# A DeltaNet scan that takes the state's part from the values before the inverse is applied, in three steps between thirds of projections

## The chip, the cores and the metric

The kernel runs on one core of one Trainium2 chip. The metric is device time in microseconds (us), from the start of the program to its end on that core. Each kernel is run several times; the median counts, and one further execution is profiled.

## The reference, cut to what matters

The reference is one layer of a decoder on 1,024 tokens of width 1,024: a gated DeltaNet with 8 heads of width 128, a sparse attention, two gates and a feed-forward part. The change touches the DeltaNet. Each head works through its sequence in chunks and hands a 128 x 128 state from chunk to chunk:

```python
kb = k * beta[..., None]
vb = v * beta[..., None]
a = jnp.where(strict, jnp.einsum('nbhid,nbhjd->nbhij', kb, k) * decay, 0.0)
t_mat = a + jnp.eye(C, dtype=f32)
u = lax.linalg.triangular_solve(t_mat, vb, left_side=True, lower=True)
w = lax.linalg.triangular_solve(t_mat, kb * jnp.exp(gc)[..., None], left_side=True, lower=True)
...
def step(state, inp):
    qd, ke, u_c, w_c, qk_c, gl = inp
    v_new = u_c - jnp.einsum('bhcd,bhde->bhce', w_c, state)
    o = jnp.einsum('bhcd,bhde->bhce', qd, state) + jnp.einsum('bhij,bhje->bhie', qk_c, v_new)
    state = state * gl[..., None, None] + jnp.einsum('bhcd,bhce->bhde', ke, v_new)
    return state, o
```

Both `u` and `w` are the inverse of `t_mat` times something. So `v_new` is also the inverse times (`vb` minus the decayed keys, scaled by beta, times the state).

## The kernel before, in words

The kernel uses chunks of 128 tokens, so a head has 8 chunks, in two halves of four. TensorE multiplies in two kinds. The projections split each float32 operand into a rounded part and a rest (`hh`, `hl` of the input, `wh`, `wl` of the weights) and add three products for each of 8 slices of the contraction; a half of one projection is 24 such products of 128 x 512 into one PSUM tile `g`. The DeltaNet's own products are 128 x 128 in plain float32; the trace has two records for each of them.

All work up to the sparse attention is entered in a list `due` by `at(step, rank, function)`, sorted by step and rank, and recorded in that order; a scheduler then settles the order on each engine. One step holds one half of a projection. `head(h, s0)` enters one head: four projections (k, q, v and the gate z) in steps `s0` to `s0 + 8`, the preparation of keys, decays and the triangular inverse beside them, the inverse's last parts up to `s0 + 15`, then `u_w` at `s0 + 15.5`, the 8 calls of `chunk` half a step apart from `s0 + 16`, and the output's norm and turn (`out_norm`, `out_turn`). The next head begins at `s0 + 14`, after six steps of other projections (`fill_nb`, four steps with 256-wide products, and one `fill_rows`, two steps). So the chunks of a head stand among the next head's projections and its key preparation. The last head's chunks stand among the remaining `fill_rows`. At step `END` the pools of this stage are closed and those of the sparse attention are opened (`tail_c`, `sparse_setup`); its items begin around `FULL`.

In `u_w`, `zs` (the inverse, transposed) is multiplied with `vb` to `u` and with `kbe` to the first half of `wq`; the second half of `wq` is the query times the decays, which GpSimd computes in `k_q`. In `chunk`, TensorE multiplies `wq` with the state `St` (two products), DVE (VectorE) forms `vn` as `u` minus the first, TensorE multiplies `ke` with `vn`, DVE updates the state, and TensorE adds `qk` times `vn` to the second product. TensorE runs its instructions in their order, so a product behind `ke` waits when `vn` is late. DVE does too. The norm of the keys (`k_natural`) goes from DVE to GpSimd for a power (`rsqrt`, line 239) and back to DVE for `nat`, and DVE's later rows stand behind `nat`.

Of the kernel before, what the change touches and what calls it, by code (L numbers as in the profile page):

```python
# [19 lines left out]
S = 1024  # L20
# [123 lines left out]
def body(ctx: ExitStack, tc: tile.TileContext, A, out):  # L144
# [246 lines left out]
    eg = PL.cq.tile([128, 8, NT], F32, name="eg")  # L391
# [3 lines left out]
    beg = PL.cq.tile([128, 8, NT], F32, name="beg")  # L395

    def gating():
# [44 lines left out]
        act(eg, gc, AF.Exp)  # L442
        V.tensor_tensor(beg, beta, eg, OP.mult)
# [187 lines left out]
    def head(h, s0):  # L631
# [11 lines left out]
        def conv(s, half):  # L643

            c0 = 20 + (s * 8 + h) * 4
            ps = H.pop("g")
            proj(ps, H["w", s], half, (4, 8))
# [30 lines left out]
        def k_turn(half):  # L678
# [6 lines left out]
            kb = t4("kbe", 2)  # L685
            rows_by(kb, kn, beg[:, h, sl])
            H["kbe", half] = kb
# [5 lines left out]
            H["qk", half] = dt = t4("qk", 3)  # L693
# [59 lines left out]
        def k_q(half):  # L753
            ac = H.pop(("ac", 0, half))
            dt = H["qk", half]
            V.tensor_tensor(dt, dt, four(H["kT", half], ac), OP.mult)
            w = pd.tile([128, 4, 2, 128], F32, name="wq", bufs=2)
            GP.tensor_tensor(w[:, :, 1], ac, H["gcB"].rearrange("p (t c) -> p t c", c=128)[:, S4[half]],
                             OP.mult)
            H["wq", half] = w  # L760

        def v_natural(half):
            ps = flip(H.pop(("ac", 2, half)))
            v_ = t4("vb", 2)
# [3 lines left out]
        def first(s, half):  # L768
            H["g"] = gtile()
            proj(H["g"], H["w", s], half, (0, 4))  # L770

        def gate(half):
            ps = H.pop("g")
            proj(ps, H["w", 3], half, (4, 8))
# [56 lines left out]
        def u_w(half):  # L831
            u = t2("u", 2)
            act(u, four(zs[half], H["vb", half]))
            H["u", half] = u
            act(H["wq", half][:, :, 0], four(H["kbe", half], zs[half]))

        def chunk(c):
# [40 lines left out]
        for i, s in enumerate((1, 0, 2, 3)):  # L878
            at(s0 + 2 * i - 2, 2, prep, s)
            for half in range(2):  # L880
                at(s0 + 2 * i + half, 1, first, s, half)
                if s < 3:
                    at(s0 + 2 * i + half + 0.5, 1, conv, s, half)
                else:
                    at(s0 + 2 * i + half + 0.5, 1, gate, half)
        for half in range(2):
# [12 lines left out]
            at(s0 + 15.5, 0, u_w, half)  # L899
        at(s0 + 5, -1, row_decay)  # L900
        at(s0 + 6.5, 0, blocks)
        for c in range(8):
            at(s0 + 16 + c / 2, -2, chunk, c)
        at(s0 + 19, -1, out_norm, 0)
        at(s0 + 20, -1, out_turn, 0)
        at(s0 + 21.2, -1, out_norm, 1)
        at(s0 + 22.2, -1, out_turn, 1)

    def fill_rows(src, dst):
# [6 lines left out]
        def begin(half):  # L916
            w[1] = gtile()
            proj(w[1], w[0], half, (0, 4))

        def go(half):  # L920
            ps = w[1]
            proj(ps, w[0], half, (4, 8))
# [5 lines left out]
        def plan(s, half):  # L928
            at(s, 1, begin, half)
            at(s + 0.5, 1, go, half)  # L930
# [3 lines left out]
    def fill_nb(u):  # L934
# [11 lines left out]

        def go(t):
            tk = slice(t * 128, (t + 1) * 128)
            ps = gtile(256)
            gemm(ps, [(hh[:, k, tk], hl[:, k, tk], w[k // 2][0][:, k % 2], w[k // 2][1][:, k % 2])  # L950
                      for k in range(8)])
# [28 lines left out]
        def plan(s, j):  # L980
            for t in (2 * j, 2 * j + 1):
                at(s + t % 2 / 2, 1, go, t)
# [8 lines left out]
    for h in range(NDN):  # L991
# [3 lines left out]
        fills = gts if h == 7 else nbs[6:] if h == 6 else [nbs[h], gts.pop(0)]  # L995
# [5 lines left out]
    END, FULL = last + 24, last + 28  # L1001
# [769 lines left out]
```

## Time and profile before

| | |
|---|---|
| Median of 3 runs | 2360.92 us (2360.64 to 2361.92) |
| The profiled execution's own time | 2355.1 us |
| Its span in the trace | 2353.3 us |
| TensorE (PE) busy | 2306.0 us, 98% |
| DVE busy | 1567.3 us, 67% |
| ScalarE (ACT) busy | 1155.6 us, 49% |
| GpSimd (POOL) busy | 184.2 us, 8% |
| Mean granted clock | 0.997 of full speed |

The span covers the recorded instructions; the profiled execution lasted 1.8 us longer, and the median of the timed runs is 5.8 us above that execution. The DeltaNet's heads take the trace from about 60 to 1035 us. The page counts a product as busy until its modelled end, which overlaps the next product's start. What one product costs in a row of products is therefore the distance between starts, not the duration shown.

### The profile page before, as it was taken

The page shows a single profiled execution, that of the slowest core. Times are in us where ns is not written, and L with a number is a line of the kernel's source. Part 1 is how long each engine was busy: PE and PEld are TensorE (multiplying, and loading weights), DVE is VectorE, ACT ScalarE, POOL GpSimd, SP SyncE. Part 2 cuts the span into 40 slices and gives each one's busy share as a digit, 9 for nine tenths or more (in the row PEclk, how much of TensorE's full clock was granted, in tenths as well). Part 3 has the DMA queues.
Part 4 walks back from the last instruction along what each step waited for, and adds up shares of the span by engine and source line. Part 5 has one row for each costly group of instructions (what it writes and reads, how often), then busy time and mean ns, then how long its engine had stood idle before and what let it go on. Part 6 is the DMA issues. An engine that isn't in the chain of part 4 may idle for free.

```text
span 2353.3 us, 43197 instructions
## 1 busy us (share of the span) xinstructions
PE 2306.0 (98%) x16257; PEld 1917.6 (81%) x16257; DVE 1567.3 (67%) x3742; ACT 1155.6 (49%) x2482; POOL 184.2 (8%) x198
## 2 busy tenths in 40 slices
PE   8999999999999999999999999999999999999999
PEld 5888988888988898886777777778878888888887
DVE  7676654747574748247777777645498777787775
ACT  4335353535444454337666666532465555544443
POOL 1021210101111121000010111100000000000000
PEclk9999999999999999999999999999999999999999
DMA  6421313131213221247342422065525443595333
GB/s 196 122 62 59 81 52 96 47 89 47 84 47 84 59 74 55 82 143 184 109 128 63 122 87 66 19 220 166 174 90 179 148 148 131 189 327 185 115 114 103
DMA packets 237378, 267.28 MB, mean 114 GB/s; under 512 B 76848, under 2 KB 128496, under 8 KB 237040
## 3 DMA queue, kind: packets, MB, share of 16 engines
q1 hardware_dynamic: 237168, 264.51, 36.1%
q8 instruction: 128, 2.10, 0.4%
q14 instruction: 82, 0.67, 0.1%
HBM read 190.02 MB, written 72.38 MB: 112 GB/s over the span
## 4 chain that ended last, share of the span: by engine, by line
PE 86%; DVE 6%; DMA 2%; issue 2%; ACT 1%; POOL 1%; SPq 0%; ACTq 0%; POOLq 0%; DVEq 0%
PE g L174 31%; PE V L174 20%; PE Q L174 12%; PE T L174 5%; PE s L174 5%; PE o L174 5%; PE S L174 2%; PE c L174 2%; PE m L174 1%; POOL ss L239 1%; PE tp L606 1%; DVE wl L274 1%; PE tp L174 1%; DVE junk L1238 0%; DVE acc L659 0%
## 5 line engine op out<-in xcount | busy, mean ns | idle before, releaser
L174 PE MATMUL g<-hh,wh 128*128 128x512 f32 (+1 forms) x816 | 335.9, 412 | 6.6 <-ACT hh L171 6.5
L174 PE MATMUL g<-hl,wh 128*128 128x512 f32 (+1 forms) x816 | 322.8, 396 | 0.1
L174 PE MATMUL g<-hh,wl 128*128 128x512 f32 (+1 forms) x816 | 322.4, 395 | 0.0
L171 ACT ACTIVATE wh<-a 128x512 fp32r<-128x512 f32 x234 | 146.5, 629 | 252.9 <-PE V L174 154.4
L174 PE MATMUL V<-big,wh 128*128 128x512 f32 x768 | 236.7, 390 | 0.8 <-DVE c L1613 0.8
L1238 DVE CUSTOM_DVE_ANT_0 junk<-S,cst 128x384 f32<-128x384 f32 (+3 forms) x320 | 168.5, 533 | 57.9 <-PE S L174 53.7
L171 ACT ACTIVATE P<-T 128x512 f32<-128x512 f32 x228 | 133.8, 597 | 102.1 <-PE T L174 89.3
L174 PEld LDWEIGHTS g<-hh,wh 128*128 128x128 f32 (+1 forms) x816 | 154.1, 189 | 36.4 <-ACT hh L171 7.1
L171 ACT ACTIVATE wh<-wr 128x512 fp32r<-128x512 f32 x168 | 105.7, 629 | 158.6 <-PE g L174 126.9
L183 DVE TENSOR_TENSOR wl<-a,wh 128x512 fp32r<-128x512 f32 x192 | 132.0, 690 | 75.2 <-ACT wh L171 74.9
L174 PEld LDWEIGHTS g<-hh,wl 128*128 128x128 f32 (+1 forms) x816 | 153.8, 188 | 33.7 <-issue 0.6
L174 PEld LDWEIGHTS g<-hl,wh 128*128 128x128 f32 (+1 forms) x816 | 154.3, 189 | 28.7 <-DVE hl L327 1.5
L174 PEld LDWEIGHTS V<-big,wh 128*128 128x128 f32 x768 | 144.1, 188 | 31.4 <-DVE c L1613 1.2
L174 PE MATMUL V<-big,wl 128*128 128x512 f32 x384 | 149.5, 389 | 0.9 <-DVE wl L274 0.9
L174 PE MATMUL g<-wh,hh 128*128 128x256 f32 x512 | 148.8, 291 | 0.3 <-DVE acc L777 0.3
L174 PE MATMUL g<-wl,hh 128*128 128x256 f32 x512 | 145.4, 284 | 0.0
L174 PE MATMUL g<-wh,hl 128*128 128x256 f32 x512 | 144.7, 283 | 0.0
L174 PEld LDWEIGHTS o<-vv,P 128*64 128x64 f32 x3648 | 115.9, 138 | 27.0 <-issue 19.4
L174 PE MATMUL o<-vv,P 128*64 128x65 f32 x3648 | 129.9, 225 | 0.6 <-DVE bs L1285 0.6
L274 DVE TENSOR_TENSOR wl<-wr,wh 128x512 fp32r<-128x512 f32 x136 | 94.1, 695 | 52.5 <-ACT wh L171 46.8
L174 PE MATMUL S<-ks,qc 96*128 96x384 f32 (+3 forms) x320 | 126.4, 407 | 1.0 <-DVE mx L1238 0.4
L174 PE MATMUL Q<-big,wh 128*128 128x512 f32 x384 | 118.4, 390 | 0.7 <-ACT wh L171 0.5
(383 smaller groups left out, 5348.9 us busy)
## 6 DMA issues: line engine op xcount, KB each, us to landing
bb<-acd SPq DMA_DIRECT2D x112, 256.0 KB, 2.7
wr<-in_w_dn_dram SPq DMA_DIRECT2D x64, 256.0 KB, 3.0
a<-in_w_u_dram SPq DMA_DIRECT2D x64, 256.0 KB, 2.7
acd<-c SPq DMA_DIRECT2D x64, 256.0 KB, 2.1
a<-in_w_d_dram SPq DMA_DIRECT2D x64, 256.0 KB, 3.7
wr<-in_w_nb_dram SPq DMA_DIRECT2D x32, 256.0 KB, 2.6
wr<-in_w_gt_dram SPq DMA_DIRECT2D x32, 256.0 KB, 2.8
gtd<-fx SPq DMA_DIRECT2D x32, 256.0 KB, 2.4
```

Of the source, the lines that this page charges most:

```text
L171: return SC.activation(o, i, fn, **kw)
L174: return PE.matmul(o, l, r, start=start, stop=stop, skip_group_check=True)
L183: V.tensor_tensor(lo, src, f(hi), OP.subtract)
L239: GP.tensor_tensor(o, o, mhalf[:ss.shape[0], :n], OP.pow)
L274: V.tensor_tensor(wl, wr, f(wh), OP.subtract)
L606: PE.transpose(pt[:, i, :], src[:, i, :], ident)
L1238: V.tensor_tensor_reduce(junk[:, :w], ps[:, :w], mask[:, a:b], 1.0, 3e38, OP.add, OP.min, o)
```

## The change

`u_w` goes, and with it `u`, `kbe` and the query half of `wq` on GpSimd. Two tiles come instead, both made on DVE in `k_q`: `kg`, the transposed keys times the decays, and `qg`, the queries times the decays. A chunk is now three functions. `chunk_keys` multiplies `kg` with the state, and DVE forms `t` as that times beta minus `vb`. `chunk_values` multiplies the inverse `zs` with `t`, and ACT copies the negated result to `vn`. `chunk_out` does the products with `ke`, `qg` and `qk` and updates the state. Each half projection is cut into 9, 9 and 6 products where it was 12 and 12, and the three functions stand between these parts. A chunk takes one step, not half a step. The output's norm and turn, `END` and `FULL` come later by one to three steps within the head, head 0 loses its `fill_rows` and the last head has one more.

```diff
-            kb = t4("kbe", 2)
-            rows_by(kb, kn, beg[:, h, sl])
-            H["kbe", half] = kb
...
-            w = pd.tile([128, 4, 2, 128], F32, name="wq", bufs=2)
-            GP.tensor_tensor(w[:, :, 1], ac, H["gcB"].rearrange("p (t c) -> p t c", c=128)[:, S4[half]],
-                             OP.mult)
-            H["wq", half] = w
+            for n, x in (("kg", H["kT", half]), ("qg", ac)):
+                H[n, half] = w = t4(n, 2 if n == "kg" else 3)
+                V.tensor_tensor(w, x, H["gcB"].rearrange("p (t c) -> p t c", c=128)[:, S4[half]], OP.mult)
...
-        def first(s, half):
-            H["g"] = gtile()
-            proj(H["g"], H["w", s], half, (0, 4))
+        def first(s, half, k):
+            if k == 0:
+                H["g"] = gtile()
+            proj(H["g"], H["w", s], half, (k, k + 3))
...
-        def u_w(half):
-            u = t2("u", 2)
-            act(u, four(zs[half], H["vb", half]))
-            H["u", half] = u
-            act(H["wq", half][:, :, 0], four(H["kbe", half], zs[half]))
-
-        def chunk(c):
+
+        def chunk_keys(c):
+            half, i = c // 4, c % 4
+            H["A"] = p = PL.pc.tile([128, 2, 128], F32, name="c")
+            if c:
+                mm(p[:, 0], H["kg", half][:, i], H["S"], True, True)
+                H["t"] = t = PL.p2.tile([128, 128], F32, name="t", bufs=2)
+                V.scalar_tensor_tensor(t, p[:, 0], beta[:, h, c:c + 1], H["vb", half][:, i],
+                                       op0=OP.mult, op1=OP.subtract)
+
+        def chunk_values(c):
+            half, i = c // 4, c % 4
+            p = H["A"]
+            mm(p[:, 1], zs[half][:, i], H["t"] if c else H["vb", half][:, i], True, True)
+            H["vn"] = vn = PL.p2.tile([128, 128], F32, name="vn", bufs=2)
+            act(vn, p[:, 1], AF.Copy, scale=-1.0 if c else 1.0)
+
+        def chunk_out(c):
             half, i = c // 4, c % 4
             if i == 0:
                 H["o", half] = t2("o", 2)
-            o, u, St = H["o", half], H["u", half], H.get("S")
-            ps = PL.pc.tile([128, 2, 128], F32, name="c")
-            if St is None:
-                vn = u[:, i]
-            else:
-                wq = H["wq", half]
-                mm(ps[:, 0], wq[:, i, 0], St, True, True)
-                mm(ps[:, 1], wq[:, i, 1], St, True, False)
-                vn = PL.p2.tile([128, 128], F32, name="vn", bufs=2)
-                V.tensor_tensor(vn, u[:, i], ps[:, 0], OP.subtract)
+            vn, St, k = H["vn"], H.get("S"), H["A"][:, 0]
+            p = PL.pc.tile([128, 128], F32, name="c")
             if c < 7:
-                p2 = PL.pc.tile([128, 128], F32, name="c")
-                mm(p2, H["ke", half][:, i, :], vn, True, True)
+                mm(k, H["ke", half][:, i, :], vn, True, True)
                 H["S"] = Sn = PL.p2.tile([128, 128], F32, name="St", bufs=2)
-                if St is None:
-                    V.tensor_copy(Sn, p2)
+                if c:
+                    V.scalar_tensor_tensor(Sn, St, H["gl"][:, c:c + 1], k, op0=OP.mult, op1=OP.add)
                 else:
-                    V.scalar_tensor_tensor(Sn, St, H["gl"][:, c:c + 1], p2, op0=OP.mult, op1=OP.add)
-            mm(ps[:, 1], H["qk", half][:, i], vn, St is None, True)
-            act(o[:, i, :], ps[:, 1], AF.Copy, scale=H["rq", half][:, i:i + 1])
+                    V.tensor_copy(Sn, k)
+            if c:
+                mm(p, H["qg", half][:, i], St, True, False)
+            mm(p, H["qk", half][:, i], vn, c == 0, True)
+            act(H["o", half][:, i, :], p, AF.Copy, scale=H["rq", half][:, i:i + 1])
...
         for c in range(8):
-            at(s0 + 16 + c / 2, -2, chunk, c)
-        at(s0 + 19, -1, out_norm, 0)
-        at(s0 + 20, -1, out_turn, 0)
-        at(s0 + 21.2, -1, out_norm, 1)
-        at(s0 + 22.2, -1, out_turn, 1)
+            for j, fn in enumerate((chunk_keys, chunk_values, chunk_out)):
+                at(s0 + 15 + (2 + j) / 3 + c + 0.001, -2, fn, c)
+        at(s0 + 20, -1, out_norm, 0)
+        at(s0 + 21, -1, out_turn, 0)
+        at(s0 + 24, -1, out_norm, 1)
+        at(s0 + 25, -1, out_turn, 1)
...
-        fills = gts if h == 7 else nbs[6:] if h == 6 else [nbs[h], gts.pop(0)]
+        fills = gts if h == 7 else nbs[6:] if h == 6 else nbs[:1] if h == 0 else [nbs[h], gts.pop(0)]
...
-    END, FULL = last + 24, last + 28
+    END, FULL = last + 26, last + 30
```

The first place is on TensorE in the scan of head 1, where a chunk of that head stands among the key preparation of head 2. Before, these rows follow each other: `wq` with the state, then three products for head 2, then `ke` and `qk` with the new `vn`.

```order
L174 MATMUL c_3621<-St_3595,wq_2502 128x128 x2
L174 MATMUL s_3645<-acc_3401,kT_3424 128x128 x3
L174 MATMUL c_3626<-vn_3624,ke_2319 128x128
L174 MATMUL c_3621<-vn_3624,qk_2326 128x128
L174 MATMUL s_3645<-acc_3401,kT_3424 128x128
L174 MATMUL s_3653<-kT_3544 128x128 x4
L174 MATMUL tp_3669<-cst0_114,tmp_3667 128x1 x4
```

With the change the same engine has, in the scan of the same head, the product with `zs`, nine projection products (the three kinds shown stand three times), the three products of `chunk_out`, six projection products, and the next `kg`.

```order
L174 MATMUL c_3473<-t_3475,zs0_420 128x128
L174 MATMUL g_3515<-hh_153,wh_3242 128x512
L174 MATMUL g_3515<-hl_154,wh_3242 128x512
L174 MATMUL g_3515<-hh_153,wl_3243 128x512
...
L174 MATMUL c_3473<-vn_3526,ke_2058 128x128
L174 MATMUL c_3537<-St_3452,qg_2235 128x128
L174 MATMUL c_3537<-vn_3526,qk_2065 128x128
...
L174 MATMUL c_3560<-St_3539,kg_2317 128x128
```

What moved: every pair of dependent products has at least six projection products between it, where before there could be as few as three small ones or three projection products.

The second place is on DVE in the scan of head 1, where the keys of head 2 are normed. Before, `vn` stands right behind `nat`, and `nat` waits for GpSimd's power of `ss`.

```order
L238 TENSOR_SCALAR ss_3344<-ss_3344 128x4
L659 SCALAR_TENSOR_TENSOR acc_3322<-xp_3319,cols_96,acc_3322 128x512
L675 TENSOR_TENSOR nat_3348<-tp_3337,ss_3344 128x512
L850 TENSOR_TENSOR vn_3378<-u_3281,c_3375 128x128
L663 SCALAR_TENSOR_TENSOR acc_3322<-xp_3319,acc_3322 128x512
L858 SCALAR_TENSOR_TENSOR St_3382<-St_3333,gl_2410,c_3380 128x128
```

With the change the state's update stands three rows behind `nat` of the second half, and `t` further behind.

```order
L668 TENSOR_REDUCE ss_3317<-tmp_3315 128x4
L655 SCALAR_TENSOR_TENSOR acc_3280<-xp_3277,cols_96,acc_3280 128x512
L238 TENSOR_SCALAR ss_3317<-ss_3317 128x4
...
L671 TENSOR_TENSOR nat_3321<-tp_3310,ss_3317 128x512
L274 TENSOR_TENSOR wl_3435<-wr_3432,wh_3434 128x512
L659 SCALAR_TENSOR_TENSOR acc_3280<-xp_3277,acc_3280 128x512
L851 SCALAR_TENSOR_TENSOR St_3347<-St_3267,gl_2224,c_3287 128x128
L648 MEMSET xp_3463 128x3
L752 TENSOR_TENSOR qg_3488<-acc_3280,gcB_2964 128x512
L650 TENSOR_TENSOR xp_3358<-g_3323,rr_163 128x512
L831 SCALAR_TENSOR_TENSOR t_3370<-c_3368,beta_401,vb_2445 128x128
```

What moved: the row that TensorE waits for behind `nat` is the state's update now, not `vn`; `vn` has left DVE for ACT.

The third place is SyncE's queue (SP) at the end of the stage, where the constants of the sparse attention (`cst2`) are loaded behind the last head's output (`odd`). Before:

```order
L875 DMA odd_142<-of_10935 128x512
L199 DMA cst2_11004<-in_cst2_dram 128x2196
L926 DMA gtd_144<-fx_10950 128x512
L1044 DMA junk_11019<-in_cst2_dram 128x512
L1050 DMA junk_11024<-in_kcc_dram 128x256
```

With the change:

```order
L872 DMA odd_142<-of_10891 128x512
L284 DMA wr_11838<-in_w_pd_dram 128x512
L199 DMA cst2_10944<-in_cst2_dram 128x2196
L925 DMA gtd_144<-fx_10919 128x512
L1056 DMA junk_10959<-in_cst2_dram 128x512
```

What moved: a load of weights stands ahead of the constants now.

## Rows read from the trace of the kernel before

**Rows 1.** The page: busy time of each engine, the chain's shares, one group of ACT.

```profile
PE 2306.0 (98%) x16257; PEld 1917.6 (81%) x16257; DVE 1567.3 (67%) x3742; ACT 1155.6 (49%) x2482; POOL 184.2 (8%) x198
...
PE 86%; DVE 6%; DMA 2%; issue 2%; ACT 1%; POOL 1%; SPq 0%; ACTq 0%; POOLq 0%; DVEq 0%
...
L171 ACT ACTIVATE wh<-a 128x512 fp32r<-128x512 f32 x234 | 146.5, 629 | 252.9 <-PE V L174 154.4
```

**Rows 2.** What PE waited for, whole span: total us, times, longest us.

```profile
PE c L174 <- DVE vn L850: 9.2, 13, 0.8
...
PE c L174 <- DVE xp L652: 4.4, 6, 0.8
...
PE s L174 <- DMA za<-xzs: 1.4, 3, 0.7
```

**Rows 3.** PE in order of time at one `u_w`: start us, us, what, records.

```profile
204.16 1.05 PE L174 MATMUL s<-vb,zs 128*128 128x128 f32 x8
...
206.90 1.06 PE L174 MATMUL s<-zs,kbe 128*128 128x128 f32 x8
207.71 0.48 PE L174 MATMUL g<-hh,wh 128*128 128x512 f32 x1
208.02 0.39 PE L174 MATMUL g<-hl,wh 128*128 128x512 f32 x1
```

**Rows 4.** PE in order of time around one product between projection products.

```profile
247.30 0.38 PE L174 MATMUL c<-vn,qk 128*128 128x128 f32 x2
247.43 0.48 PE L174 MATMUL g<-hl,wh 128*128 128x512 f32 x1
247.75 0.40 PE L174 MATMUL g<-hh,wl 128*128 128x512 f32 x1
```

**Rows 5.** PE in order of time in one chunk; idle time and releaser in brackets.

```profile
214.19 0.61 PE L174 MATMUL c<-St,wq 128*128 128x128 f32 x4
214.55 0.48 PE L174 MATMUL g<-hh,wh 128*128 128x512 f32 x1
...
215.79 0.40 PE L174 MATMUL g<-hh,wl 128*128 128x512 f32 x1
216.87 0.49 PE L174 MATMUL c<-vn,ke 128*128 128x128 f32 x2 [0.68 <-DVE vn L850]
```

**Rows 6.** DVE in order of time in the same chunk.

```profile
214.15 0.17 DVE L238 TENSOR_SCALAR ss<-ss 128x4 f32<-128x4 f32 x1
...
215.93 0.69 DVE L675 TENSOR_TENSOR nat<-tp,ss 128x512 f32<-128x512 f32 x1 [0.90 <-POOL ss L239]
216.53 0.28 DVE L850 TENSOR_TENSOR vn<-u,c 128x128 f32<-128x128 f32 x1
```

**Rows 7.** The chain of waits in the last head: start us, us, what, records.

```profile
1001.75 0.44 PE c L174 x4
...
1006.70 0.64 PE c L174 x4
```

**Rows 8.** Operations on tile `c`: count, ns at least, median, at most.

```profile
L171 ACT ACTIVATE o<-c,rq x64: 342/360/369, 211.2 to 1018.9; 128x128 f32<-128x128 f32 x64
...
L850 DVE TENSOR_TENSOR vn<-u,c x56: 272/278/290, 216.5 to 1018.0; 128x128 f32<-128x128 f32 x56
L858 DVE SCALAR_TENSOR_TENSOR St<-St,gl,c x48: 340/348/350, 217.4 to 1014.7; 128x128 f32<-128x128 f32 x48
```

**Rows 9.** GpSimd's power of `ss`, from the operations on that tile.

```profile
L239 POOL TENSOR_TENSOR ss<-ss,mhalf x16: 1006/1436/1497, 111.4 to 900.7; 128x4 f32<-128x4 f32 x16
```

**Rows 10.** PE in order of time at the change to the sparse attention.

```profile
1034.38 0.60 PE L606 MATMUL c<-cst,o 128*128 128x128 f32 x4
...
1048.46 0.28 PE L174 MATMUL m<-far,gsel 128*128 128x256 f32 x1
```

**Rows 11.** DVE in order of time there: the cast that `m` reads.

```profile
1046.63 0.29 DVE L1052 CAST far<-junk 128x256 fp32r<-128x256 f32 x1
```

**Rows 12.** PE in order of time at the inverse of one head.

```profile
497.36 1.09 PE L174 MATMUL s<-za,n 64*64 64x64 f32 x16 [0.72 <-DMA za<-xzs]
```

More of the change, by code (lines that the diff above doesn't have):

```diff
@@ L390, in body @@
     gc = PL.cq.tile([128, 8, NT], F32, name="gc")
-    eg = PL.cq.tile([128, 8, NT], F32, name="eg")
     ek = PL.cq.tile([128, 8, NT], F32, name="ek")
@@ L394, in body @@
     hbeta = PL.cq.tile([128, 8, NT], F32, name="hbeta")
-    beg = PL.cq.tile([128, 8, NT], F32, name="beg")
     def gating():
@@ L441, in gating @@
         act(ek, ek, AF.Exp)
-        act(eg, gc, AF.Exp)
-        V.tensor_tensor(beg, beta, eg, OP.mult)
         pg = PL.pc.tile([64, 128], F32, name="c")
@@ L646, in conv @@
             ps = H.pop("g")
-            proj(ps, H["w", s], half, (4, 8))
+            proj(ps, H["w", s], half, (6, 8))
             xp = pd.tile([128, 515], F32, name="xp", bufs=2)
@@ L692, in k_turn @@
             V.tensor_tensor(ut, H["gcB"].rearrange("p (t c) -> p t c", c=128)[:, sl], b3(gc[:, h, sl]), OP.subtract)
-            H["qk", half] = dt = t4("qk", 3)
+            H["qk", half] = dt = t4("qk", 4)
             V.tensor_tensor(dt, ut, bm("m2"), OP.add)
@@ L880, in head @@
             for half in range(2):
-                at(s0 + 2 * i + half, 1, first, s, half)
+                for k in (0, 3):
+                    at(s0 + 2 * i + half + k / 9, 1, first, s, half, k)
                 if s < 3:
-                    at(s0 + 2 * i + half + 0.5, 1, conv, s, half)
+                    at(s0 + 2 * i + half + 2 / 3, 1, conv, s, half)
                 else:
-                    at(s0 + 2 * i + half + 0.5, 1, gate, half)
+                    at(s0 + 2 * i + half + 2 / 3, 1, gate, half)
         for half in range(2):
@@ L898, in head @@
             at(s0 + 15, 0, last_x, half)
-            at(s0 + 15.5, 0, u_w, half)
         at(s0 + 5, -1, row_decay)
@@ L914, in prep, with begin @@
             w[0] = unit(src)
-        def begin(half):
-            w[1] = gtile()
-            proj(w[1], w[0], half, (0, 4))
+        def begin(half, k):
+            if k == 0:
+                w[1] = gtile()
+            proj(w[1], w[0], half, (k, k + 3))
         def go(half):
             ps = w[1]
-            proj(ps, w[0], half, (4, 8))
+            proj(ps, w[0], half, (6, 8))
             x = PL.pf.tile([128, 512], F32, name="fx", bufs=2)
@@ L928, in plan @@
         def plan(s, half):
-            at(s, 1, begin, half)
-            at(s + 0.5, 1, go, half)
+            at(s, 1, begin, half, 0)
+            at(s + 1 / 3, 1, begin, half, 3)
+            at(s + 2 / 3, 1, go, half)
         return prep, [lambda s, i=i: plan(s, i) for i in range(2)]
@@ L945, in prep, with part, begin @@
                 w.append((wh, wl))
+        def part(ps, t, ks):
+            tk = slice(t * 128, (t + 1) * 128)
+            for k in ks:
+                wh, wl = [a[:, k % 2] for a in w[k // 2]]
+                mm(ps, hh[:, k, tk], wh, k == 0, False)
+                mm(ps, hh[:, k, tk], wl, False, False)
+                mm(ps, hl[:, k, tk], wh, False, k == 7)
+        def begin(t):
+            X["g"] = gtile(256)
+            part(X["g"], t, range(4))
         def go(t):
             tk = slice(t * 128, (t + 1) * 128)
-            ps = gtile(256)
-            gemm(ps, [(hh[:, k, tk], hl[:, k, tk], w[k // 2][0][:, k % 2], w[k // 2][1][:, k % 2])
-                      for k in range(8)])
+            ps = X.pop("g")
+            part(ps, t, range(4, 8))
             x = PL.p2.tile([128, 256], F32, name="nx", bufs=4)
@@ L981, in plan @@
             for t in (2 * j, 2 * j + 1):
-                at(s + t % 2 / 2, 1, go, t)
+                at(s + t % 2 / 2, 1, begin, t)
+                at(s + t % 2 / 2 + 0.25, 1, go, t)
                 if u not in (2, 3):
```

4 lines of the change are left out of this document (2 added, 2 removed).

## The prediction

> **What bounds the kernel now.** I read the page first. TensorE (PE) is busy 98% of the span and holds 86% of the chain that ended last; DVE with 67% and ACT with 49% have room on average [rows 1]. So a change counts in two ways only: by the products that PE must do, and by the time in which PE stands still. Then I read what PE waits for [rows 2]. Of its own stage the scan's `vn` is the largest wait: 13 times for 9.2 us, and 6 times for 4.4 us that the trace puts down to an `xp` that stands beside `vn` on DVE. Together that is 13.6 us in 19 of 56 chunks. The inverse's load `za` comes to 1.4 us in 3 waits. Next I read PE in order of time at one `u_w` [rows 3], in one chunk [rows 5], and DVE in that chunk [rows 6]: the first `wq` pair starts at 214.19, six projection products cover 1.4 us, and `ke` still waits 0.68 us, since `vn` stands behind `nat`, and `nat` stood idle 0.90 us for GpSimd's power. The chain is late because a short wait on another path sits in front of it on an engine that runs in order.
>
> **Fewer products.** `u_w` has 16 float32 products of 128 x 128 in each head: 32 records from 204.16 to 207.71 us, and the projection product behind them starts its successor 0.31 us later where 0.23 is usual, so 3.63 us, or 0.227 us for one [rows 3]. (0.23 is the distance in the run of projection products from 214.55 to 215.79: 1.24 us for five, of which the first took 0.32 [rows 5].) The new form spreads such products singly between projection products. One that stands alone costs 247.43 - 247.30 = 0.13 us plus the 0.09 us by which the next distance, 0.32, is above 0.23: 0.22 us [rows 4]. Cutting the halves in thirds thus costs nothing beyond the products. Count for a head: 16 in `u_w` and 29 in the chunks before (2 in the first, 4 in six of them, 3 in the last); 37 after (3, six times 5, 4). That is 8 fewer in a head, 64 in all, **14.3 us** less (14.1 at 0.22, 14.5 at 0.227). The cuts of the projections, the move of one `fill_rows` from head 0 to the last head, and the later steps of the norm add no product.
>
> **The waits that go.** The 13.6 us [rows 2] should go where the chain has more cover. Behind these lie waits too short to be counted, since a product's modelled end covers 0.16 us of them: in the last head a pair costs 0.44 us without one and `ke` with `qk` 0.64 with one [rows 7]. 37 chunks at most 0.2 us bound this from 0 to 4 us once the many chunks with long cover are left out; I take **2 us**, in the middle, since both kinds are frequent.
>
> **The waits that come.** A chunk now has three crossings: `kg` with the state, DVE's `t`, `zs` with `t`; then ACT's `vn`, `ke`; then DVE's state, the next `kg`. Two are covered by nine projection products, 2.05 us. The third has `qg`, `qk` and six products, 0.45 + 1.37 = 1.8 us. `t` and the state's update are of one kind with today's update, 0.35 us, and `vn` on ACT like its output rows, 0.36 us [rows 8]. ACT may have a 0.63 us pass under way [rows 1] and one more behind it, 1.6 us with `vn`: still below 2.05. `t` stands behind `xp`, about 0.7 + 0.35 us, against 2.05. So `t` and `vn` should not be waited for.
>
> The state's update is the narrow one, because it has taken `vn`'s place behind `nat`. By hand, from the end of the turn that feeds the second `nat`: PE needs 2.05 + 0.22 + 2.05 us to `ke` and its product, so the update can begin at 4.55 and the next `kg` wants it at 6.4. DVE's rows before it are: the sum behind ACT's square (0.63 [rows 1]), two `acc` rows, GpSimd's power of 1.0 to 1.5 us [rows 9], `nat`, then `wl`, `acc` and the update at 0.35; a DVE row of 512 columns is taken at `nat`'s 0.69 or a little less [rows 6]. Started at once that ends near 5.95, 0.45 us early. With two ACT passes ahead of the square (1.3 us) it ends 0.9 us late. Two such places in each of 7 heads, at 0.3 us each, make **4 us** (from 0 to 15: the upper end is 19 waits of 0.8 us, as many and as long as today's longest).
>
> **The other moved work.** `kbe` (8 ACT rows in a head), the copies of `u` and `wq` and GpSimd's product go; DVE gets `kg` and `qg`, four operations of about 0.69 us in a head. All of that lies beside PE's work; without cover DVE's 32 operations would be 22 us. At the stage's end the output's last turn stands one step before the pools close, not 1.8, and a step is 24 x 0.23 = 5.5 us: up to 4.4 us less time for the sparse attention's constants. In the order, 56 projection products lie between that turn and `m`, where there were 60, and the constants' load waits behind one more weight load. Today the cast that `m` reads ends at 1046.92 and `m` starts at 1048.46 us [rows 10, 11], 1.5 us to spare. I take **1.5 us** of loss (0 to 4.4). For `za`, one wait of 0.72 us [rows 12] shows that a head's inverse has nothing to spare. Three of the previous head's chunks now stand in its stretch: 15 products, 3.3 us more cover on PE, against three `t`, two updates, one `kg` and one `qg`, 3.1 us, in DVE's queue. I take 0 (-1.4 to the rival below).
>
> **A rule against the change.** GpSimd's power of `ss` takes 1.01 us at its shortest and 1.44 at the median [rows 9]; the long one of rows 6's chunk ran beside an `acc` row of DVE with two SBUF inputs.
> The Trainium skill, "SBUF — State Buffer", section "SBUF: two separate sides", says that DVE and GpSimd share a pair of SBUF ports as an exclusive lock: a DVE operation with two SBUF inputs and a GpSimd operation that reads SBUF shut each other out for a whole instruction. The trace agrees with it in that 1.01 to 1.44; no run here yet shows `kg` or `qg` beside a power. `kg` and `qg` are operations with two SBUF inputs, while the old product's lock on GpSimd's side goes.
> If each of the 14 overlapped powers became 0.5 us longer (1.50 less 1.01 [rows 9]) and `nat` and the update were late by all of it, the loss would be 7 us. The median is already near the maximum, so I leave it out of the sum.
>
> **Sum.** -14.3 - 13.6 - 2 + 4 + 1.5 = -24.4 us, against the profiled execution's 2355.1: 2330.7. The median of the runs is 5.8 above that execution, so about 2337 us.
>
> **The rivals.** *The waits come back*: `nat` stays in front, now of the state, and 13.6 us of new waits replace the old ones. For it: the row order is the same but for the name. Against: 1.8 us of cover where six products gave 1.4. Then 2360.9 - 14.3 + 1.5 = 2348. *Everything fits*: no new wait, constants in time: -14.3 - 13.6 - 4 = 2329. *The ports*: 2337 + 7 = 2344. *No change*: 19 to 29 us of new waits beyond the forecast's own, at 24 about four in every seven overlapped chunks at 0.8 us; nothing in today's rows is that frequent (19 in 56). *The inverse is late, and it is slower*: DVE runs in order, so the chain of small operations that leads to `za` now waits for each `t` and each update of the previous head until PE has come to it. Today's spare is none [rows 12]. Five such rows a head; when each is 1 us too early in the queue, the chain is 5 us late, 35 us over 7 heads, and the time is 2372. It decides from 29 us, 4.2 us a head; below that the change still gains. Against it: the PE work in that stretch grows as much as DVE's.
>
> **How the numbers follow.** Forecast 0.60, ports 0.06, waits back 0.15, everything fits 0.07, no change 0.06, slower 0.06. The range from 2328 to 2351 holds the first four (the sums with all low and all high ends are 2327 and 2352). A measurement here can tell about 0.2%, 4.7 us, from no change: faster 0.88, within 0.06, slower 0.06.
>
> **What would show it.** Right: the profile after has no `vn` in PE's waits, few waits for `St`, 64 fewer 128 x 128 products (128 records), and PE's waits inside the scan come to well under 13.6 us. The update behind `nat` should be the row waited for where any is. Wrong: PE waits for `St` or ACT's `vn` in most chunks; the wait for `za` above 2 us a head; `m` waiting for `far` by more than 4 us; or PE's distance between projection products above 0.23 us.

## The result and the profile after

The changed kernel takes 2328.86 us (median of 4, 2328.3 to 2329.85), the kernel before 2361.28 us beside it (2360.64 to 2361.92): 0.9863 of the time, with an interval from 0.9846 to 0.988, or 32 us less. Its profiled execution lasted 2329.85 us and spans 2328.1 us; against the profiled execution of before, 2355.1 us, that is 25.2 us less. The forecast was 2337 us in a range from 2328 to 2351. One of five executions of the run with `vn` on DVE, below, lasted 3200 us at a mean granted clock of 0.654, where all others have 0.993 to 0.998; its ratio leaves that one out.

The page, in the order of [rows 1]: engines' busy time, then the chain's shares.

```profile
PE 2287.5 (98%) x16129; PEld 1903.8 (82%) x16129; DVE 1579.2 (68%) x3773; ACT 1138.1 (49%) x2449; POOL 165.5 (7%) x182
...
PE 85%; DVE 7%; DMA 2%; ACT 2%; issue 2%; POOL 1%; SPq 0%; ACTq 0%; POOLq 0%; DVEq 0%
```

TensorE (PE) has 128 records less, 64 products, as counted. It is still what bounds the kernel. What it waited for, beside [rows 2]:

```profile
PE c L174 <- ACT vn L171: 2.9, 6, 1.0
...
PE m L174 <- issue: 1.3, 1, 1.3
...
PE c L174 <- DVE St L851: 1.2, 6, 0.3
```

In the scan 13.6 us of waits have become 4.1 us: six for `vn`, which is on ACT now, and six for the state. No wait for `za` is left. The operations on tile `c` and GpSimd's power, beside [rows 8] and [rows 9]:

```profile
L171 ACT ACTIVATE vn<-c x64: 250/277/279, 214.5 to 998.5; 128x128 f32<-128x128 f32 x64
...
L831 DVE SCALAR_TENSOR_TENSOR t<-c,beta,vb x56: 332/342/346, 219.0 to 996.5; 128x128 f32<-128x128 f32 x56
L851 DVE SCALAR_TENSOR_TENSOR St<-St,gl,c x48: 330/342/350, 226.6 to 994.1; 128x128 f32<-128x128 f32 x48
```

```profile
L239 POOL TENSOR_TENSOR ss<-ss,mhalf x16: 1380/1494/1503, 113.2 to 859.6; 128x4 f32<-128x4 f32 x16
```

The power's shortest rose from 1.01 to 1.38 us. At the change of stage, beside [rows 10], PE has:

```profile
1007.58 0.60 PE L602 MATMUL c<-cst,o 128*128 128x128 f32 x4
...
1022.26 0.35 PE L174 MATMUL m<-far,gsel 128*128 128x256 f32 x1 [1.34 <-issue]
```

The last turn starts 26.8 us earlier (1034.38 to 1007.58), `m` 26.2 us earlier, and the end comes 25.2 us earlier. To compare the same work, the stage is taken from the start of one and the same projection product (the 241st of 512 columns, at 109.94 us before and 111.47 us after) to the last turn. Before and after, by the windows view (span; busy time of PE, PEld, DVE, ACT, POOL; clock; DMA):

```profile
109.94:1034.38 924.44, 907.86 (x6775) 791.67 (x6774) 545.38 (x1321) 415.11 (x939) 126.54 (x112) 1.00 0.24 68
```

```profile
111.47:1007.58 896.11, 890.31 (x6659) 778.44 (x6658) 557.00 (x1353) 397.64 (x908) 107.60 (x96) 1.00 0.25 71
```

The stage is 28.3 us shorter: 10.8 us of that are PE's idle time (16.6 to 5.8), 17.5 us busy time. It has 116 records less, not 128, since twelve projection products that stood behind the last turn before (four ahead of `m`, eight behind it) now stand in the stage. At 0.23 us each they are 2.8 us, so for the same work the stage is 31.1 us shorter.

Outside the stage time is lost. The trace is 1.5 us later when the stage begins; two profiles of the kernel before differ by 1.2 us there. The way from the turn to `m` is 0.6 us longer with four products less, and what follows `m` 0.9 us longer with eight products less. In the 80 us behind the turn the granted clock stands at one half of full speed, its lower level of 1.2 GHz, for 10.2 us, before for 3.4 us (in the second profiles of the two kernels, below, for 6.8 and not at all).

### The profile page after: what moved, and what is told of

The parts are those of the page before. It is cut to its first block, busy times and chain, and to the rows that moved or that the text cites. A ratio compares the mean times of both kernels' runs of the same rounds, so it can differ in the third digit from the quotient of the medians.

```text
span 2328.1 us, 42886 instructions
## 1 busy us (share of the span) xinstructions
PE 2287.5 (98%) x16129; PEld 1903.8 (82%) x16129; DVE 1579.2 (68%) x3773; ACT 1138.1 (49%) x2449; POOL 165.5 (7%) x182
## 3 DMA queue, kind: packets, MB, share of 16 engines
q8 instruction: 127, 2.08, 0.4%
## 4 chain that ended last, share of the span: by engine, by line
PE 85%; DVE 7%; DMA 2%; ACT 2%; issue 2%; POOL 1%; SPq 0%; ACTq 0%; POOLq 0%; DVEq 0%
PE g L174 30%; PE V L174 20%; PE Q L174 12%; PE T L174 5%; PE o L174 5%; PE s L174 4%; PE c L174 3%; PE S L174 2%; PE m L174 1%; PE tp L602 1%; DVE acc L655 1%; POOL ss L239 1%; PE tp L174 1%; DVE wl L274 0%; PE tp L982 0%
```

## The experiments

Every kernel was timed beside the kernel before. "Stage" is the time from the 241st projection product of 512 columns (at 109 to 112 us) to the last turn of the DeltaNet, "idle" the part of it in which PE isn't busy, "to m" the time from that turn to the first `m`. The stage of the kernel before and of "algebra alone" holds twelve projection products less than the others (2.8 us). On the way to `m` these two have 36 projection products, most have 32, "key norm, stage's end" and "three moves" 27, and the last two 24.

| kernel | median us | ratio to before (interval) | stage | idle | to m |
|---|---|---|---|---|---|
| before, first profile | 2361.3 | 1 | 924.4 | 16.6 | 14.1 |
| before again | 2359.0 | 1.000 (0.9991 to 1.0009) | 924.3 | 16.3 | 14.1 |
| changed | 2328.9 | 0.9863 (0.9846 to 0.988) | 896.1 | 5.8 | 14.7 |
| changed again | 2328.8 | 0.9864 (0.9851 to 0.9878) | 896.3 | 6.1 | 14.9 |
| spacing alone | 2359.9 | 0.9999 (0.9989 to 1.001) | 925.9 | 13.4 | 17.9 |
| algebra alone | 2352.0 | 0.9966 (0.9954 to 0.9978) | 919.0 | 15.1 | 14.2 |
| products back | 2338.5 | 0.9912 (0.9898 to 0.9926) | 906.4 | 3.6 | 15.4 |
| `vn` on DVE | 2343.0 | 0.9918 (0.9905 to 0.9932) | 907.6 | 13.7 | 17.3 |
| output norm later | 2331.6 | 0.9874 (0.9859 to 0.9889) | 895.6 | 4.5 | 18.2 |
| key norm later | 2326.1 | 0.986 (0.9847 to 0.9874) | 894.8 | 5.2 | 16.4 |
| key norm, stage's end | 2324.4 | 0.9853 (0.984 to 0.9867) | 894.6 | 5.0 | 14.2 |
| three moves | 2323.5 | 0.9844 (0.9831 to 0.9857) | 893.2 | 2.9 | 13.9 |
| `far` first | 2327.9 | 0.9873 (0.9851 to 0.9896) | 896.3 | 6.0 | 12.9 |
| all moves | 2328.3 | 0.9868 (0.9843 to 0.9893) | 896.8 | 6.4 | 14.8 |

**The two kernels once more.** No edit.

> The kernel before, unchanged, profiled once more. My forecast added 5.8 us to its sum, because the first profiled execution of this kernel (2355.1 us) lay that far below its median. Theory A, that first profiled execution was a fast one: this one is profiled near 2361 us, and the extra 6 us stand in a few stretches of the trace outside the scan. Theory B, profiling makes this kernel faster each time: profiled near 2355 again, with timed runs near 2361. The scan's waits are 13.6 us in 19 places under both.

> The changed kernel as it is, as the measure for the three beside it on the same chip. If its runs spread as those of the kernel before do (2355 to 2365 us), the 32 us of the result carry some luck; if they stay within 1 or 2 us of 2329, the spread belongs to the kernel before.

Measured: before was profiled at 2359.04 us, its median; 25 timed runs of it on that chip lie between 2355.2 and 2365.3. So theory A holds: the first profiled execution was one from the low end. Its scan waits are the same 13.6 us. The other 4 us lie outside the stage, which is as long as in the first profile (924.3 to 924.4 us): 1.2 us ahead of it and 2.9 us behind `m`. The changed kernel ran from 2326.1 to 2331.6 in four runs, so the result isn't luck, but its spread isn't as small as the first four runs had it.

**Spacing alone.** The old `chunk` in two functions, one chunk a step, between thirds of projections; `u_w` and the old products stay, the query product on GpSimd too.

```diff
-            at(s0 + 16 + c / 2, -2, chunk, c)
+            at(s0 + 16 + c + 0.001, -2, chunk_state, c)
+            at(s0 + 16 + c + 1 / 3 + 0.001, -2, chunk_out, c)
```

> The old products (u, w, two products with the state) in the new places: one chunk in a step, in two parts between thirds of projections. Counted in the new order of the products, 1.4 to 4.3 us of other products now lie between the product with the state and the one that reads vn, where the kernel before has 0.7 to 2.1. Forecast's theory, the two terms are separate: the 13.6 us of waits and some of the 2 us of hidden ones go, the 14.3 us of products stay, about 1.5 us are lost at the change of stage: 2361 - 14 = 2347 us. Rival, the gain is all in the products and spacing alone does little: 2357 to 2361. Rival, the waits were the larger part: 2340 or less.

Measured: no gain in the time. The first rival holds as to the time, though not as to its reason (see the next experiment). The trace says why. PE's waits (total us, times, longest) in the stage:

```profile
PE c L174 <- DVE vn L849: 6.6, 6, 1.9
PE tp L606 <- DVE acc L663: 2.7, 5, 0.6
```

And one of the waits for `vn`, on DVE, GpSimd and PE:

```profile
587.41 1.49 DVE L984 TENSOR_TENSOR nx<-nx,fss 128x256 f32<-128x256 f32 x1 [1.12 <-POOL fss L239]
588.82 0.28 DVE L849 TENSOR_TENSOR vn<-u,c 128x128 f32<-128x128 f32 x1
```

```profile
586.37 1.01 POOL L239 TENSOR_TENSOR fss<-fss,mhalf 128x4 f32<-128x4 f32 x1 [2.12 <-DVE fss L238]
587.34 1.27 POOL L758 TENSOR_TENSOR wq<-acc,gcB 128x512 f32<-128x512 f32 x1
```

```profile
589.15 0.49 PE L174 MATMUL c<-vn,qk 128*128 128x128 f32 x2 [1.16 <-DVE vn L849]
```

DVE stands 1.12 us for a power, then its `nx` row takes 1.49 us where 0.42 to 0.43 is usual (all 48 in the kernel before), while GpSimd's product with the decays runs beside it. Together that is 2.6 us ahead of `vn`, more than a cover of 1.4 to 2.05 us. So the wait on another path comes back through the next row that has one. `acc` is late in a similar way: three rows of `kbe`, 0.99 us, stand on ACT ahead of the pass that it waits for. Besides, 3.8 us were lost at the change of stage. PE's busy time in the stage rose by 4.4 us against before again: 2.8 us are the twelve projection products, and about 1.5 us come from the granted clock, which stands at one half for 3.4 us right behind the longest wait for `vn` (1.88 us, to 257.09):

```profile
257.60:261.00 3.40, 3.40 (x18) 3.40 (x18) 2.26 (x12) 0.67 (x2) 1.01 (x1) 0.51 0.00 0
```

The 256-column products come 0.21 us apart there, where 0.12 is usual. So spacing alone is worth about 1 us in the stage for the same work, and the change of stage takes it back. `qk` has three buffers here, as in the kernel before, where the changed kernel has four.

**Algebra alone.** The new products in the old places, halves cut 12 and 12.

```diff
+        def chunk(c):
+            chunk_keys(c)
+            chunk_values(c)
+            chunk_out(c)
```

> The new products (kg, zs with t, 8 fewer in a head) in the old places: half a step for a chunk, halves of projections cut 12 and 12, no gap asked for between the three parts. Counted in its order, only 0.44 to 0.9 us of other products lie between the product with zs and the one that reads vn in all 48 places, and under 1.2 us in 24 of 56 places for t. Theory of spacing: the third crossing from engine to engine is not covered; 48 waits of 0.3 to 0.6 us and some for t and the state, 20 to 35 us, against 14 us of products: 2365 to 2382 us, slower than before. Rival, fewer products are what counts wherever they stand: 2347 us with waits no longer than today's 13.6.

Measured: 2352.0 us, 7 us faster than before. My theory had the sign wrong, and the rival had too much gain. The waits are 13.3 us, as long as before, of new kinds:

```profile
PE c L174 <- ACT vn L171: 7.3, 7, 1.1
...
PE c L174 <- DVE t L834: 6.0, 13, 0.5
```

I had 48 waits for `vn`; seven are shown, yet it was late in every place, mostly by too little to be counted as idle. A product that was late shows in the distance to the one behind it:

```profile
228.32 0.46 PE L174 MATMUL c<-vn,ke 128*128 128x128 f32 x2
228.61 0.39 PE L174 MATMUL c<-vn,qk 128*128 128x128 f32 x2
```

0.29 us to `qk`, where the changed kernel has 0.22 from one product to the next. In this kernel that distance is over 0.26 us in 56 of 56 places, in the kernel before in 40 of 48, in the changed one behind `ke` in 6 of 56. In all 56 places `ke` starts 0.05 to 0.08 us behind the end of `vn`. The stage of this kernel has 13.7 us more busy time than the changed kernel's (904.0 to 890.3), and that with twelve projection products less, so 16.5 us for the same work. Not all of it is waits that no idle time shows. Behind three of the six waits of 1.1 us for `vn` the granted clock stands at one half, for 10.2 us together, and projection products come 0.43 us apart, where 0.23 is usual:

```profile
238.98 0.49 PE L174 MATMUL c<-vn,ke 128*128 128x128 f32 x2 [1.10 <-ACT vn L171]
...
241.45 0.63 PE L174 MATMUL g<-hh,wh 128*128 128x512 f32 x1
241.88 0.63 PE L174 MATMUL g<-hl,wh 128*128 128x512 f32 x1
```

```profile
241.20:244.60 3.40, 3.40 (x10) 2.62 (x9) 2.60 (x8) 0.63 (x1) 0.67 (x1) 0.50 0.23 38
```

That costs about 4.7 us and leaves about 12 us of unseen waits. In the scans of the kernel before and of the changed one the clock stays at full speed.

**Products back.** The first product of the output is done twice.

```diff
+                mm(p, H["qg", half][:, i], St, True, True)
                 mm(p, H["qg", half][:, i], St, True, False)
+            else:
+                mm(p, H["qk", half][:, i], vn, True, True)
```

> The changed kernel with 64 float32 products of 128 x 128 put back, 8 in a head: in each chunk the first product of the output is done twice, the first time for nothing. They stand behind the product with ke, so the state's update and vn are waited for no longer. Forecast's theory: 0.22 us each, 14 us: 2329 + 14 = 2343 us. Rival, a lone product between projections hides in the weight load beside it and costs about 0.13 us: 2337. Rival, the gain did not come from the products: 2329 to 2331.

Measured: 9.6 us more by the medians and 10.3 us in the stage, between the theories. The price of a product is the forecast's:

```profile
344.18 0.61 PE L174 MATMUL c<-St,qg 128*128 128x128 f32 x4
344.63 0.39 PE L174 MATMUL c<-vn,qk 128*128 128x128 f32 x2
```

0.45 us for two, where one takes 0.22; 64 of them are 14.4 us. PE's busy time in the stage rose by 12.5 us and its idle time fell by 2.2, since every product more is cover for the next wait (`vn` 2.9 to 0.9 us). So the price was right, and taking products away gives back more than a quarter of it in waits when the chain is tight.

**`vn` on DVE.**

```diff
-            act(vn, p[:, 1], AF.Copy, scale=-1.0 if c else 1.0)
+            V.tensor_scalar(vn, p[:, 1], -1.0 if c else 1.0, None, op0=OP.mult)
```

> The changed kernel with vn copied from PSUM by DVE, not ACT; nothing else. The scheduler orders the rows anew. Forecast's theory: each crossing has 1.4 to 2.05 us of cover, so the engine hardly matters: 2327 to 2333. Rival, from the run with the new spacing alone (its vn stood on DVE behind rows that wait for GpSimd's powers, up to 1.9 us late): vn leaving DVE is what makes the spacing work; then 1 to 2 waits a head of 0.5 to 1.2 us come back: 2334 to 2345.

Measured: 2343 us. The rival holds. The waits of the scan are back:

```profile
PE c L174 <- DVE vn L839: 6.9, 12, 2.1
...
PE c L174 <- DVE xi L719: 4.6, 5, 0.9
```

14 us by the medians for one row's engine, with spacing and products unchanged (the order of the other rows isn't, since the scheduler settles it anew). In the traces 11.4 us of it lie in the stage; about 1.5 of these are the clock, at one half for 3.4 us behind the longest wait for `vn` (2.08 us). Another 2.6 us are lost on the way to `m`.

**Output norm later.**

```diff
-        at(s0 + 20, -1, out_norm, 0)
+        at(s0 + 20.4, -1, out_norm, 0)
-        at(s0 + 21, -1, out_turn, 0)
+        at(s0 + 21.4, -1, out_turn, 0)
```

> The changed kernel with the first half's output norm and its turn entered 0.4 of a step later, behind the fifth chunk's last part. Theory: in the changed kernel the six waits for vn (2.9 us shown) come from that norm: its four rows on ACT wait for GpSimd's power, take 1.28 us, and vn stands behind them. Then the six waits go, and with what a product's modelled end covers and the slower product behind a wait about 0.25 us each more: 3 to 4.5 us, 2329 becomes 2325 us. Rival, it is ACT's load as a whole that makes vn late: the waits move to other chunks, no gain. Second rival, the turn now comes later than its readers want: 2329 or a little more.

The wait it was to remove, in the changed kernel on ACT and PE:

```profile
342.03 1.28 ACT L171 ACTIVATE o<-o,oss 128x128 f32<-128x128 f32 x4 [1.99 <-POOL oss L239]
343.22 0.26 ACT L171 ACTIVATE vn<-c 128x128 f32<-128x128 f32 x1
```

```profile
343.53 0.49 PE L174 MATMUL c<-vn,ke 128*128 128x128 f32 x2 [0.35 <-ACT vn L171]
```

Measured: all six waits for `vn` went, so the cause is shown. Five waits of 0.31 to 0.38 us came for the next `kg`, four of them put down to ACT's `o`:

```profile
343.30 0.70 ACT L171 ACTIVATE o<-o,oss 128x128 f32<-128x128 f32 x2 [0.47 <-POOL oss L239]
343.90 0.35 ACT L171 ACTIVATE o<-c,rq 128x128 f32<-128x128 f32 x1
```

```profile
344.30 0.49 PE L174 MATMUL c<-St,kg 128*128 128x128 f32 x2 [0.31 <-ACT o L171]
...
1025.16 0.55 PE L174 MATMUL m<-far,gsel 128*128 128x256 f32 x1 [4.91 <-DMA rb<-nsd]
```

The norm's rows now stand ahead of the row that empties the PSUM tile which `kg` writes next. The stage is 0.7 us shorter than in the changed kernel run again, and `m` then waits 4.9 us: the whole is 2.9 us slower. The rival's first half was right. The wait for `m` costs more than its length, since the granted clock falls to one half during it and stays there behind it:

```profile
1023.20:1030.00 6.80, 4.84 (x12) 3.83 (x13) 6.51 (x17) 1.57 (x2) 0.00 (x0) 0.50 0.84 182
```

In the five runs in which `m` waits longest (3.05 to 4.91 us: spacing alone, `vn` on DVE, output norm later, key norm later, all moves) the clock falls during that wait or within 1 us behind it. In the others it is at full speed there.

**Key norm later, and with the stage's end.**

```diff
-            at(s0 + 2 + half, 0, k_natural, half)
+            at(s0 + 2 + half + (0.4 if half and h else 0), 0, k_natural, half)
```

```diff
-    END, FULL = last + 26, last + 30
+    END, FULL = last + 25.4, last + 30
```

> The changed kernel with one of the three moves alone: the second half's key norm, from head 1 on, enters 0.4 of a step later. Theory: six waits for the state's update (1.2 us shown, 0.25 more each for what a modelled end covers and the slower product behind a wait) go, since nat and the power that it waits for no longer stand ahead of the update: 2.5 us, 2329 becomes 2326 us; vn's six waits stay. Rival, the key norm is on the way to the inverse, which comes late: 2330 or more. Second rival, the gain of the three moves together was mostly this one: 2324 or 2325.

> The later key norm and the earlier change of stage, without the later output norm. Theory: the output norm's later place gained nothing by itself (six waits for vn went, five for the state behind ACT's rows came), so this one is as fast as the three together, 2323 to 2325 us. Rival, the later output norm counts once the others are moved: 2326 us. The product m should wait 1 to 2 us, since the earlier change of stage gave about 1 us in the run with three moves.

> The changed kernel with three entries moved: the first half's norm and turn 0.4 of a step later, the second half's key norm (from head 1 on) 0.4 of a step later, so that the state's update doesn't stand behind nat, and the change of stage 0.6 of a step earlier, so that the constants of the sparse attention are loaded earlier. If all three waits that the changed kernel still shows go (vn 2.9, St 1.2, m for far 1.3 us, and 0.25 us more for each of the first twelve): 2329 - 8 = 2321 us. Rival, the later key norm makes the inverse late, which had nothing to spare: a wait for za of 0.5 us or more in each head, 2326 or worse.

The wait for the state in the changed kernel, on DVE, GpSimd and PE:

```profile
315.23 0.16 DVE L238 TENSOR_SCALAR ss<-ss 128x4 f32<-128x4 f32 x1
315.35 0.75 DVE L655 SCALAR_TENSOR_TENSOR acc<-xp,cols,acc 128x512 f32<-128x512 f32 x1
317.00 0.69 DVE L671 TENSOR_TENSOR nat<-tp,ss 128x512 f32<-128x512 f32 x1 [0.90 <-POOL ss L239]
...
318.81 0.34 DVE L851 SCALAR_TENSOR_TENSOR St<-St,gl,c 128x128 f32<-128x128 f32 x1
```

```profile
315.47 1.50 POOL L239 TENSOR_TENSOR ss<-ss,mhalf 128x4 f32<-128x4 f32 x1 [6.56 <-DVE ss L238]
```

```profile
319.29 0.46 PE L174 MATMUL c<-St,kg 128*128 128x128 f32 x2 [0.19 <-DVE St L851]
```

Measured: with the key norm alone later the waits for the state are gone, and seven for `vn` are left (4.0 us). The stage is 1.5 us shorter than in the changed kernel run again, but the way to `m` is 1.5 us longer, with a wait of 3.05 us. The median, 2326.1 us, is 2.7 us lower, on another chip and within the spread of the executions, so the expected 2.5 us aren't shown. With the earlier end of the stage the median is 2324.4 us; five projection products have moved behind `m`, which waits 2.03 us. With the later output norm as well it is 2323.5 us. The last step lies within the runs' spread (2322.6 to 2326.3 and 2323.5 to 2327.4), though in the traces the stage is 1.4 us shorter by it. The inverse did not come late in any of them. The three moves are the fastest version found, 5.2 us below the changed kernel on the same chip.

**`far` first, and all moves.** The second kernel has the three moves too, with the output norm at 20.55.

```diff
         pn = PL.pn
+        raw = pn.tile([128, 256], F32, name="junk", bufs=2)
+        SY.dma_start(raw, A["kcc"])
+        far = pn.tile([128, 256], F32R, name="far")
+        V.tensor_copy(far, raw)
         load_consts(pn, 2)
```

> The changed kernel with the load and the cast of far entered ahead of the large load of the sparse attention's constants, nothing else. In the changed kernel the last turn of the DeltaNet starts at 1007.6 us, the large load is issued 5.0 us later and lands 10.9 us after the turn, and the cast of far ends 14.5 us after it, behind eight other casts; m waits 1.3 us (4.9 in the run with the norm later). Theory: the change of stage waits for this chain of loads and casts; with far done early only the large load is left, and m can start about 11 to 12 us behind the turn: 1 to 2 us less, 2327 to 2328 us. Rival, the product m only changes places with projection products that have to be done anyway, and the next product of the sparse attention waits for the casts instead: 2329.

> The run with three moves (2323.5 us), with the norm of the first half entered another 0.15 of a step later and far loaded and cast first. In that run kg still waited five times for 0.31 us behind two rows of the norm on ACT, which stood ahead of the row that empties the PSUM tile. If the rows of the norm now fall between that row and the next vn, the five waits go: 1.6 us shown and 0.25 each more, 3 us, and far gives 1 us: 2320 us. Rival, the norm's rows come to stand before the sixth chunk's vn and it waits instead: 2322 to 2324.

Measured: `far` first shortens the way from the turn to `m` by 1.8 us (14.7 to 12.9), and the span by 1.1; the median is 0.9 us lower, less than the spread. The trace speaks for the rival: eight projection products, 1.8 us, have changed places with `m`, which waits 1.55 us, and what follows `m` is 1.4 us longer. With all moves together the stage is 3.6 us longer than with three, and neither theory had the place:

```profile
348.52 0.66 PE L602 MATMUL c<-cst,o 128*128 128x128 f32 x4 [0.77 <-DVE St L851]
```

The turn, moved with the norm, waits 0.77 us in five heads, and `m` waits 3.5 us.

## Why the prediction held, and where it did not

**The saving was too small, and a low base hid it.** The forecast saved 24.4 us. The medians give 32.4 (2361.3 to 2328.9 us) and 31.7 on another chip, so the time came out only 0.9 us above the range's lower end. The sum, 2330.7 us, is 0.9 us above the changed kernel's profiled execution, but that is luck. It starts from an execution at the low end of the spread of the kernel before; the second profile of that kernel lasted 2359.0 us, with a span 4.0 us longer and the same waits in the scan. So the 5.8 us of the last addition were in place, and the saving is what was short. Between the second profiles of the two kernels it is 29.0 us (spans of 2357.3 and 2328.3), 4.6 more than the forecast. About 4 of these are the unseen waits, below. The other 3 us that the medians show lie within the spread of the executions and stay open. The rival *Everything fits* has 2329 us, by luck as well: it has no new wait, and there are twelve.

**Fewer products** held: 128 records, 64 products at 0.225 us each (0.45 for two in the run with products back), 14.4 us (forecast 14.3).

**The waits that go** held for those that the trace shows, though not in reason. All 13.6 us of `vn`'s waits on DVE went. But I put that down to cover, and spacing alone gained nothing: DVE's rows can be 2.6 us late behind GpSimd. The waits went because the chain got cover and `vn` left the engine that waits for GpSimd; with `vn` on DVE 14 us come back, and with the old spacing 13.3 us of other waits stay.

The 2 us of unseen waits were mis-sized: "37 chunks at most 0.2 us bound this from 0 to 4 us". Of the stage's 17.5 us of busy time 14.4 are products, and twelve products, 2.8 us, came in; that leaves about 6 us. I had looked for unseen waits only in the chunks without a shown one, but a shown wait hides about 0.25 us as well. And there were more late chunks than I thought: 40 of 48 in the kernel before, of which 18 show idle time at `ke`. In these 40 `ke` starts 0.05 to 0.17 us behind the end of `vn`, in the other eight 0.21 us or later.

**The waits that come** held as a sum, 4.1 us for 4, by luck, since they are of another kind. For the state I had 14 places of 0.3 us; there are six of 0.2 to 0.3. "So `t` and `vn` should not be waited for" failed for `vn`: I counted ACT's passes of 0.63 us but not the four rows of the output norm, 1.28 us, which wait for a power of GpSimd's. In the first overlapped head, besides, the cover is twelve products of 256 columns, 1.4 us, where I had 2.05; there the wait is 1.0 us.

**The handover** held: `m` waits 1.34 us, and its way from the turn is 1.5 us longer for the same work (forecast 1.5). In the experiments with the changed kernel's products `m` waits 1.3 to 4.9 us, so this term was worth its range of 4.4 us. What the clock costs behind `m` the forecast did not have.

**The inverse**: no wait for `za` is left, so "0" and the rival's low chance were right. One sentence of that rival is off: "below that the change still gains" holds below 24 us of lateness by its own numbers, not below 29.

**The ports.** I left the rule out since the power's median was near its maximum. It lengthened all the same: none of the 16 powers of `ss` takes 1.01 us now, where seven did. It isn't `kg` or `qg` but the row order that does it. A power that begins 0.12 us behind an `acc` row with two SBUF inputs takes 1.50 us; in the run with three moves the second half's stands beside `xp`, one of whose inputs is in PSUM:

```profile
315.81 0.68 DVE L650 TENSOR_TENSOR xp<-g,rr 128x512 f32<-128x512 f32 x1
```

```profile
315.99 1.01 POOL L239 TENSOR_TENSOR ss<-ss,mhalf 128x4 f32<-128x4 f32 x1 [10.22 <-DVE ss L238]
```

And with the spacing alone it went the other way round: `nx`, two SBUF inputs, took 1.49 us beside GpSimd's product. The Trainium skill, "SBUF — State Buffer", section "SBUF: two separate sides", has the pair of ports that DVE and GpSimd share as an exclusive lock, which whoever starts first holds for a whole instruction. Both traces agree, in both directions. What it cost here is little, not the 7 us of the rival. Of what PE waits for, only the update behind `nat` hangs on a power of `ss`: PE waits 1.2 us for `St`, and without these waits, in the run with the key norm later, the stage is 1.5 us shorter. The waits for `vn` hang on the power of `oss`, and that one still takes 1.01 us in 13 of 16 places.

## What to carry to other kernels

Cover on the bounding engine is worth only as much as the engine that has to answer is free of waits of its own: put the step that the chain waits for on an engine whose queue doesn't wait for a third one, then space it. Two edits can each be worth little and much together (here 0 and 7 us alone, 32 us together), so price them with the row that will stand in front, not one by one. A wait that a trace shows is worth more than its idle time, so count what it hides as well. And judge a forecast by its saving: a sum that starts from one low execution can meet the time while the saving is 8 us short.

## What the runs showed of the hardware

- A product of 128 x 128 that waited makes the next one come 0.29 to 0.33 us later, where 0.22 is usual, and the first 0.16 us of a wait lie under the modelled end of the product before: a wait costs about 0.25 us more than the trace calls idle, and 22 of 40 late chunks in the kernel before show no idle time at `ke` at all.
- Behind five of the scan's longest waits (1.1 to 2.1 us, in spacing alone, algebra alone and `vn` on DVE) the granted clock stood at one half, 1.2 GHz, for 3.4 us each; products of 512 columns came 0.43 us apart there and not 0.23, those of 256 columns 0.21 and not 0.12. Behind three other waits of 1.1 us in algebra alone it stayed at full speed.
- GpSimd's power of four columns takes 1.01 us or up to 1.50 by what DVE has begun 0.1 us earlier, and a DVE row of 256 columns 0.43 or 1.49 us by what GpSimd has begun 0.07 us earlier.
- The same kernel's runs spread over 10 us (25 of the kernel before, 2355.2 to 2365.3), and the mean granted clock goes with a part of it: three runs at 0.998 took 2355.2 to 2357.9 us, the five at 0.993 to 0.995 took 2360.3 to 2365.3. The thirteen at 0.996 still spread from 2356.9 to 2363.9; what makes those differ stays open.
